# Residual and first product put into PSUM by ScalarE, so that the matmuls add to them

## The chip, the cores and the metric

The kernel runs on one core of a Trainium2 chip. The metric is the device time of one execution in microseconds (us); times are medians of several runs. A traced execution gives the profile: the busy time of TensorE (PE), its weight load (PEld), VectorE (DVE), ScalarE (ACT), GpSimd (POOL), and the DMA queues, of which SyncE (SP) issues nearly all.

## The reference

Two layers over 256 tokens of width 1024. Each layer has a token mixer beside a cross-attention, and then the dense channel mixer with which the change deals:

```python
def layer_norm(x, g, b): ...       # over the last axis
def swiglu(x, w_in, w_out):
    g, u = jnp.split(x @ w_in, 2, axis=-1)
    return (jax.nn.silu(g) * u) @ w_out
for i in range(DEPTH):             # DEPTH = 2
    ...
    x = layer_norm(ALPHA * x + sub, ln_mix_g[i], ln_mix_b[i])
    x = layer_norm(ALPHA * x + swiglu(x, w_ffn_in[i], w_ffn_out[i]), ln_ffn_g[i], ln_ffn_b[i])
```

Everything is float32. w_ffn_in[i] is 1024 x 5632 and w_ffn_out[i] is 2816 x 1024.

## The kernel before

**Tiling.** The 256 tokens are two tiles of 128 (tt = 0, 1). The 2816 hidden columns are eleven chunks of 256. Each float32 operand is split into two parts that TensorE multiplies: the high part is a cast on ScalarE (L240), the low part is the rest, a subtraction on VectorE (L241). Three matmul passes (PASSES) make one product. So each half of a weight unit, 128x1024, costs one cast, one subtraction and its matmuls. Weight units come from memory as 1 MB loads (`raw_...`) through a ring of four; the split halves (`spl_...`) go through a ring of ten.

**Channel mixer.** Class Ffn. PLANS says which chunks are plain ("R", chunk_in) and which pairs of chunks are made with seven products M1 to M7 in Strassen's manner ("S", product). In layer 0 the pairs begin at chunks 2, 4, 6, 8; in layer 1 at 3, 5, 7, 9. A pair needs sums of raw weight blocks: two adds of 128x2048 on VectorE (L195) beside one accumulating load by POOL, and a third add for M4. The names of tiles carry f for layer 0 and g for layer 1.

**A pair, step by step.** M1 is copied by ScalarE from its bank X to SBUF (m1). M5 is copied to m5. When M2 is done in bank Y, VectorE adds it to m1 (L611) and ScalarE applies Silu. M6 is copied to u2, VectorE adds M3 to it (L615) and multiplies it with m1 (L616). M7, again in bank X, is added to m5 by VectorE (L618); after that M4 may overwrite the bank. ScalarE makes sg = Silu(M4) (L621), VectorE multiplies m5 by it (L622). The results m1 and m5 are transposed by TensorE at the next "tp" step (L644), and the transposed tiles tp are split by L240 and L241 into ht (htf, htg), the left operand of the output matmuls (chunk_out, acc_mms) into four accumulator banks fo (fof, fog): two token tiles by two halves of 512 columns.

**LayerNorm.** When a tile's sums are complete, VectorE computes ALPHA*xres + fo into xres (L338), bn_stats of it (L344), the aggregate (L350), adds epsilon (L352); POOL takes the power; two more VectorE operations per piece normalise (L356, L357). In the last tile (last_tile) the sums of the last three chunks go to three extra banks `last`, which VectorE adds to xres (L717), column piece by column piece.

**Order.** TensorE's order is written by hand (manual_schedule; ffn_steps makes it). The orders of the other engines and of SP's queue are set by a scheduler from the whole program, so an edit at one place can move instructions at others.

Of the kernel before, what the change touches and what calls it, by code (L numbers as in the profile page):

```python
# [21 lines left out]
P = 128  # L22
# [8 lines left out]
LAST_PIECES = ((0, 512), (512, 768), (768, 1024))  # L31
PASSES = ((0, 0), (0, 1), (1, 0))
# [195 lines left out]
def build(nc, tc, ins, out):  # L228
    ET = mybir.EngineType
    with (  # L230
# [99 lines left out]
        class LayerNorm:  # L330
            def __init__(self, tt, xres, acc, nm):
                self.tt, self.r, self.acc, self.nm = tt, xres[tt], acc, nm
                self.stats = sm(f"st{nm}{tt}", 18)
                self.n = 0

            def piece(self, i):
                c0, c1 = PIECES[i]
                nc.vector.scalar_tensor_tensor(  # L338
                    self.r[:, c0:c1], self.r[:, c0:c1], ALPHA, self.acc[c0 // 512][:, c0 % 512:c0 % 512 + c1 - c0],
                    ALU.mult, ALU.add)  # L340
                self.sums(c0, c1)

            def sums(self, c0, c1):
# [149 lines left out]
        def acc_mms(acc, lhs, rhs, first, last):  # L493

            for a in range(2):
                for b in range(2 - a):
                    for h in range(2):
                        mm(acc[h], lhs(a), rhs(b, h * 512, h * 512 + 512), first and a == 0 and b == 0, last and a == 1)

        def closing(acc, terms, ln):  # L500

            for p, (c0, c1) in enumerate(PIECES):
                for i, (lhs, rhs) in enumerate(terms):
                    for a in range(2):
                        for b in range(2 - a):
                            mm(acc[c0 // 512][:, c0 % 512:c0 % 512 + c1 - c0], lhs(a), rhs(b, c0, c1),
                               False, i == len(terms) - 1 and a == 1)
                ln.piece(p)
# [24 lines left out]
        class Ffn:  # L533
# [52 lines left out]
            def product(self, c, m):  # L586


                if m == "M1":
                    self.X, self.Y, self.Z = (mm_tile(f"{n}{self.nm}{c}") for n in "XYZ")  # L590
                dst = {"M1": self.X, "M6": self.X, "M7": self.X, "M4": self.X, "M2": self.Y}.get(m, self.Z)
                alone = m in ("M1", "M5", "M2")
# [61 lines left out]
            def run(self, mid=None):  # L654
                for st in ffn_steps(self.l):
# [14 lines left out]
                    elif st[0] == "tp":  # L670
                        if self.pending:
# [10 lines left out]
            def chunk_out(self, c, k, tts):  # L682
                if c == 0 and k == 0:
                    self.alloc()
                for tt in tts:
                    acc_mms(self.acc[tt], *self.term(c, k, tt), c == 0 and k == 0,
                            self.l == 1 and c == NFF - 4 and tt == 1 and k == 1)
# [3 lines left out]
            def end_tile(self, tt, mid=None):  # L691

                for c in range(NFF - 2 if tt == 0 else NFF - 3, NFF - 1):
                    for k in range(2):
                        acc_mms(self.acc[tt], *self.term(c, k, tt), False, False)
# [4 lines left out]
                ln = LayerNorm(tt, self.xres, self.acc[tt], self.nm)  # L700
                closing(self.acc[tt], [self.term(NFF - 1, k, tt) for k in range(2)], ln)
# [4 lines left out]
            def last_tile(self, tt):  # L706

                ln = LayerNorm(tt, self.xres, self.acc[tt], self.nm)
# [313 lines left out]
```

## Time and profile before

| | us |
|---|---|
| median of 3 runs | 566.76 (566.74 to 566.94) |
| the profiled execution, its own time | 567.08 |
| span from its first to its last instruction | 565.4 |
| TensorE busy in it | 554.6 |
| VectorE busy | 499.3 |
| ScalarE busy | 360.6 |

TensorE is busy 98% of the span, at a mean granted clock of 0.995. The share of an engine is a mean over stages; what an edit is worth is read from the stage in which it stands. An instruction's row gives its start and its length; the next instruction of the same engine may start some 0.08 us before the end of the one before it, so a split of 1.22 us takes 1.13 to 1.14 us of the engine's time in a run of splits.

### The profile page before, as it was taken

The page shows a single profiled execution, that of the slowest core. Times are in us where ns is not written, and L with a number is a line of the kernel's source. Part 1 is how long each engine was busy: PE and PEld are TensorE (multiplying, and loading weights), DVE is VectorE, ACT ScalarE, POOL GpSimd, SP SyncE. Part 2 cuts the span into 40 slices and gives each one's busy share as a digit, 9 for nine tenths or more (in the row PEclk, how much of TensorE's full clock was granted, in tenths as well). Part 3 has the DMA queues.
Part 4 walks back from the last instruction along what each step waited for, and adds up shares of the span by engine and source line. Part 5 has one row for each costly group of instructions (what it writes and reads, how often), then busy time and mean ns, then how long its engine had stood idle before and what let it go on. Part 6 is the DMA issues. An engine that isn't in the chain of part 4 may idle for free.

```text
span 565.4 us, 8050 instructions
## 1 busy us (share of the span) xinstructions
PE 554.6 (98%) x3064; PEld 479.4 (85%) x3064; DVE 499.3 (88%) x641; ACT 360.6 (64%) x552; POOL 22.5 (4%) x32
## 2 busy tenths in 40 slices
PE   8999999999999999999999999999999999999994
PEld 8999979888888888888999998788888887888884
DVE  5796989999997999995987887589998997999986
ACT  6765957768664756872475987555676674765820
POOL 2020000000000000000100000000000000000001
PEclk9999999999999999999999999999999999999997
DMA  8995786547866576687476324237367766585602
GB/s 303 410 369 225 248 311 231 204 77 305 214 241 216 139 298 150 228 329 261 152 267 256 144 77 148 85 149 284 90 176 278 206 243 213 137 305 145 222 1 74
DMA packets 21334, 118.88 MB, mean 210 GB/s; under 512 B 2352, under 2 KB 5552, under 8 KB 8880
## 3 DMA queue, kind: packets, MB, share of 16 engines
q1 hardware_dynamic: 19856, 109.72, 52.7%
q0 software_dynamic: 1152, 8.39, 8.2%
q8 instruction: 24, 0.39, 0.3%
q10 hardware_dynamic: 288, 0.26, 0.1%
q14 instruction: 14, 0.11, 0.1%
HBM read 117.31 MB, written 1.05 MB: 209 GB/s over the span
## 4 chain that ended last, share of the span: by engine, by line
PE 85%; DVE 8%; ACT 2%; DMA 2%; issue 2%; SPq 0%; POOLq 0%; ACTq 0%; DVEq 0%
PE fof L264 11%; PE Xf L264 8%; PE fog L264 6%; PE pf L264 6%; PE pg L264 6%; PE Xg L264 5%; PE opc L264 4%; PE opa L264 4%; PE Zf L264 4%; PE qk L264 4%; PE pu L264 3%; PE bv L264 3%; PE pvm L264 3%; PE Zg L264 3%; PE va L264 3%; PE hkm L264 2%
## 5 line engine op out<-in xcount | busy, mean ns | idle before, releaser
L240 ACT CAST spl_s_M<-raw_s 128x1024 fp32r<-128x1024 f32 x112 | 114.8, 1053 | 51.3 <-DVE raw_s L195 37.3
L241 DVE TENSOR_TENSOR spl_s_M<-raw_s,spl_s_M 128x1024 fp32r<-128x1024 f32 x112 | 132.8, 1219 | 5.7 <-ACT spl_s_M L240 5.4
L264 PE MATMUL fof<-spl_w,htf 128*128 128x512 f32 x264 | 63.8, 392 | 0.0
L264 PEld LDWEIGHTS fof<-spl_w,htf 128*128 128x128 f32 x264 | 49.0, 188 | 10.0
L264 PE MATMUL fog<-spl_w,htg 128*128 128x512 f32 x228 | 55.3, 392 | 0.0
L195 DVE TENSOR_TENSOR raw_s<-raw_s,raw_s 128x2048 f32<-128x2048 f32 x24 | 54.9, 2286 | 0.2
L241 DVE TENSOR_TENSOR spl_w<-raw_w,spl_w 128x1024 fp32r<-128x1024 f32 x44 | 53.0, 1218 | 1.5 <-ACT spl_w L240 1.5
L240 ACT CAST spl_w<-raw_w 128x1024 fp32r<-128x1024 f32 x44 | 45.5, 1052 | 6.6 <-PE fog L264 1.9
L264 PEld LDWEIGHTS fog<-spl_w,htg 128*128 128x128 f32 x228 | 42.4, 188 | 8.6
L264 PE MATMUL qk<-x2T,spl_qk 128*128 128x256 f32 x288 | 36.7, 285 | 0.0
L264 PEld LDWEIGHTS qk<-x2T,spl_qk 128*128 128x128 f32 x288 | 35.2, 192 | 0.0
L264 PE MATMUL opc<-spl_o,mix 128*128 128x512 f32 x96 | 23.5, 397 | 0.0
L264 PE MATMUL Xf<-spl_s_M,SfM 128*128 128x512 f32 x96 | 23.1, 389 | 0.0
L264 PE MATMUL Xg<-spl_s_M,x3T 128*128 128x512 f32 x96 | 22.8, 391 | 0.3 <-DVE m5g L618 0.3
L264 PE MATMUL Zg<-spl_s_M,SgM 128*128 128x512 f32 x96 | 23.1, 389 | 0.0
L264 PE MATMUL Xg<-spl_s_M,SgM 128*128 128x512 f32 x96 | 23.1, 389 | 0.0
L264 PE MATMUL Zf<-spl_s_M,SfM 128*128 128x512 f32 x96 | 23.1, 389 | 0.0
L264 PE MATMUL Xf<-spl_s_M,x1T 128*128 128x512 f32 x96 | 22.6, 389 | 0.0
L264 PE MATMUL opa<-spl_o,mix 128*128 128x512 f32 x96 | 22.5, 392 | 0.0
L264 PEld LDWEIGHTS Xg<-spl_s_M,x3T 128*128 128x128 f32 x96 | 17.9, 188 | 4.5 <-DVE m5g L618 0.8
L264 PEld LDWEIGHTS Xf<-spl_s_M,SfM 128*128 128x128 f32 x96 | 18.0, 188 | 3.8
L264 PEld LDWEIGHTS Xg<-spl_s_M,SgM 128*128 128x128 f32 x96 | 18.0, 188 | 3.7
(240 smaller groups left out, 1101.9 us busy)
## 6 DMA issues: line engine op xcount, KB each, us to landing
raw_s<-in_w SPq DMA_DIRECT2D x32, 1024.0 KB, 4.8
raw_w<-in_w SPq DMA_DIRECT2D x22, 1024.0 KB, 5.6
raw_o<-in_w SPq DMA_DIRECT2D x8, 1024.0 KB, 6.7
raw_s<-in_w POOLq DMA_DIRECT2D x8, 1024.0 KB, 8.2
raw_r_A<-in_w SPq DMA_DIRECT2D x6, 1024.0 KB, 4.8
raw_r_B<-in_w SPq DMA_DIRECT2D x6, 1024.0 KB, 4.8
raw_qk<-in_w SPq DMA_DIRECT2D x6, 1024.0 KB, 5.6
raw_u<-in_w SPq DMA_DIRECT2D x3, 1024.0 KB, 8.6
```

The costliest lines, as they stand in the source:

```text
L195: self.nc.vector.tensor_add(self.raw[parts[0]], self.raw[parts[0]], self.raw[parts[1]])
L240: nc.scalar.copy(hi, src)
L241: nc.vector.tensor_sub(lo, src, hi.bitcast(F32))
L264: nc.tensor.matmul(o, lhsT, rhs, start=start, stop=stop, skip_group_check=on)
```

## The change

Three edits. First, at the first "tp" step of a channel mixer, ScalarE writes ALPHA*xres into the four accumulator banks (eight operations of 128x512 in all); every output matmul then adds to what lies there, and LayerNorm reads its sums from the banks, not from xres. The six additions of L338 that served the channel mixers, and five more of last_tile (L710, L717), are gone; last_tile adds into the banks themselves, pieces in another order. Second, ScalarE copies M1 into the bank of M2, the matmuls of M2 add to it, and Silu reads the bank: the eight adds of L611 are gone. In the new code the tile that M1, M6, M7 and M4 write is named Y, and M2's X. Third, transposes are written as plain matmul instructions with flags, four in a group; their number stays.

```diff
+            def src(self, c0, c1):
+                return self.part(c0, c1) if self.seeded else self.r[:, c0:c1]
...
             def sums(self, c0, c1):
-                nc.vector.bn_stats(self.stats[:, 6 * self.n:6 * self.n + 6], self.r[:, c0:c1])
+                nc.vector.bn_stats(self.stats[:, 6 * self.n:6 * self.n + 6], self.src(c0, c1))
...
-                    nc.vector.scalar_tensor_tensor(r[:, sl], r[:, sl], mv[:, 0:1], gb[:, 0, sl], ALU.subtract, ALU.mult)
+                    nc.vector.scalar_tensor_tensor(r[:, sl], self.src(c0, c1), mv[:, 0:1], gb[:, 0, sl], ALU.subtract, ALU.mult)
...
-            def alloc(self):
+            def seed(self):
                 self.acc = [[acc_tile(f"fo{self.nm}{tt}{h}") for h in range(2)] for tt in range(2)]
+                for tt in range(2):
+                    for h in range(2):
+                        nc.scalar.mul(self.acc[tt][h], self.xres[tt][:, h * 512:(h + 1) * 512], ALPHA)
...
-                alone = m in ("M1", "M5", "M2")
+                alone = m in ("M1", "M5")
...
                 if m == "M1":
-                    self.m1 = kept("m1", self.X)
+                    nc.scalar.copy(self.Y, self.X)
...
                 elif m == "M2":
-                    nc.vector.tensor_add(self.m1, self.m1, self.Y)
-                    nc.scalar.activation(self.m1, self.m1, AF.Silu)
+                    self.m1 = work_tile(f"m1{self.nm}{c}")
+                    nc.scalar.activation(self.m1, self.Y, AF.Silu)
...
-                            nc.tensor.transpose(tp[:, k, tt * P:(tt + 1) * P], hs[tt][:, k * P:(k + 1) * P], ident)
+                            nc.tensor.matmul(tp[:, k, tt * P:(tt + 1) * P], hs[tt][:, k * P:(k + 1) * P], ident,
+                                             start=k + tt == 0, stop=k + tt == 2, is_transpose=True, skip_group_check=True)
...
             def last_tile(self, tt):
-                ln = LayerNorm(tt, self.xres, self.acc[tt], self.nm)
-                for h, (c0, c1) in enumerate(PIECES):
-                    nc.vector.scalar_tensor_tensor(ln.r[:, c0:c1], ln.r[:, c0:c1], ALPHA, self.acc[tt][h], ALU.mult, ALU.add)
+                ln = LayerNorm(tt, self.xres, self.acc[tt], self.nm, True)
                 terms = [self.term(c, k, tt) for c in range(NFF - 3, NFF) for k in range(2)]
-                for c0, c1 in LAST_PIECES:
-                    t = mm_tile(f"last{c0}")[:, :c1 - c0]
+                for c0, c1 in LAST_ORDER:
                     for i, (lhs, rhs) in enumerate(terms):
                         for n, (a, b) in enumerate(PASSES):
-                            mm(t, lhs(a), rhs(b, c0, c1), i == 0 and n == 0, i == len(terms) - 1 and n == 2)
-                    nc.vector.tensor_add(ln.r[:, c0:c1], ln.r[:, c0:c1], t)
+                            mm(ln.part(c0, c1), lhs(a), rhs(b, c0, c1), False, i == len(terms) - 1 and n == 2, True)
                     ln.sums(c0, c1)
```

LAST_ORDER is (512, 768), (0, 512), (768, 1024).

The scheduler's orders change with it. First place: VectorE at the end of layer 0's pair 8 and the start of plain chunk 10. Before, from the add into u2 to the last product of m5 (L622):

```order
L615 TENSOR_TENSOR u2f8_2227<-u2f8_2227,Zf8_2081 128x512
L241 TENSOR_TENSOR spl_w0_7_0_2271<-raw_w0_7_2119,spl_w0_7_0_2271 128x1024
L616 SCALAR_TENSOR_TENSOR m1f8_2100<-m1f8_2100,u2f8_2227 128x512
L241 TENSOR_TENSOR spl_s0_8_M4_0_2287<-raw_s0_8_21_2064,spl_s0_8_M4_0_2287 128x1024
L241 TENSOR_TENSOR spl_s0_8_M4_1_2296<-raw_s0_8_21_2064,spl_s0_8_M4_1_2296 128x1024
L618 TENSOR_TENSOR m5f8_2153<-m5f8_2153,Xf8_2079 128x512
L241 TENSOR_TENSOR spl_r0_10_A_0_2310<-raw_r0_10_A_2258,spl_r0_10_A_0_2310 128x1024
L241 TENSOR_TENSOR spl_w0_7_1_2344<-raw_w0_7_2119,spl_w0_7_1_2344 128x1024
L241 TENSOR_TENSOR spl_r0_10_A_1_2361<-raw_r0_10_A_2258,spl_r0_10_A_1_2361 128x1024
L241 TENSOR_TENSOR spl_r0_10_B_0_2378<-raw_r0_10_B_2260,spl_r0_10_B_0_2378 128x1024
L622 SCALAR_TENSOR_TENSOR m5f8_2153<-m5f8_2153,sgf8_2305 128x512
```

Now:

```order
L629 TENSOR_TENSOR u2f8_2227<-u2f8_2227,Zf8_2082 128x512
L242 TENSOR_TENSOR spl_r0_10_A_0_2310<-raw_r0_10_A_2258,spl_r0_10_A_0_2310 128x1024
L630 SCALAR_TENSOR_TENSOR m1f8_2188<-m1f8_2188,u2f8_2227 128x512
L242 TENSOR_TENSOR spl_w0_7_1_2344<-raw_w0_7_2119,spl_w0_7_1_2344 128x1024
L242 TENSOR_TENSOR spl_r0_10_A_1_2361<-raw_r0_10_A_2258,spl_r0_10_A_1_2361 128x1024
L632 TENSOR_TENSOR m5f8_2153<-m5f8_2153,Yf8_2081 128x512
L242 TENSOR_TENSOR spl_r0_10_B_0_2378<-raw_r0_10_B_2260,spl_r0_10_B_0_2378 128x1024
L242 TENSOR_TENSOR spl_r0_10_B_1_2393<-raw_r0_10_B_2260,spl_r0_10_B_1_2393 128x1024
L242 TENSOR_TENSOR spl_w0_8_0_2416<-raw_w0_8_2262,spl_w0_8_0_2416 128x1024
L242 TENSOR_TENSOR spl_w0_8_1_2425<-raw_w0_8_2262,spl_w0_8_1_2425 128x1024
L242 TENSOR_TENSOR spl_w0_9_0_2444<-raw_w0_9_2347,spl_w0_9_0_2444 128x1024
L636 SCALAR_TENSOR_TENSOR m5f8_2153<-m5f8_2153,sgf8_2305 128x512
```

The add of M7 into m5 (L618, now L632) stood ahead of the four splits for chunk 10 and w0_7; it now stands behind three of them. The last product of m5 (now L636) stood behind one further split, and now stands behind five, the last of which is of w0_9.

Second place: VectorE at the start of layer 1's pair 9, where m5g7 is finished and htg7, htg8 are the transposed results of pair 7. Before:

```order
L618 TENSOR_TENSOR m5g7_4616<-m5g7_4616,Xg7_4542 128x512
L241 TENSOR_TENSOR spl_w1_7_0_4831<-raw_w1_7_4758,spl_w1_7_0_4831 128x1024
L195 TENSOR_TENSOR raw_s1_9_11_4756<-raw_s1_9_11_4756,raw_s1_9_12_4760 128x2048
L241 TENSOR_TENSOR spl_s1_9_M5_0_4848<-raw_s1_9_11_4756,spl_s1_9_M5_0_4848 128x1024
L622 SCALAR_TENSOR_TENSOR m5g7_4616<-m5g7_4616,sgg7_4772 128x512
L241 TENSOR_TENSOR spl_s1_9_M5_1_4857<-raw_s1_9_11_4756,spl_s1_9_M5_1_4857 128x1024
L241 TENSOR_TENSOR spl_s1_9_M2_0_4868<-raw_s1_9_21_4762,spl_s1_9_M2_0_4868 128x1024
L241 TENSOR_TENSOR htg7_4804<-tpg7_4775,htg7_4804 128x512
L241 TENSOR_TENSOR htg8_4811<-tpg8_4776,htg8_4811 128x512
L241 TENSOR_TENSOR spl_s1_9_M2_1_4877<-raw_s1_9_21_4762,spl_s1_9_M2_1_4877 128x1024
```

Now:

```order
L632 TENSOR_TENSOR m5g7_4613<-m5g7_4613,Yg7_4541 128x512
L242 TENSOR_TENSOR spl_w1_7_0_4827<-raw_w1_7_4755,spl_w1_7_0_4827 128x1024
L196 TENSOR_TENSOR raw_s1_9_11_4753<-raw_s1_9_11_4753,raw_s1_9_12_4757 128x2048
L242 TENSOR_TENSOR spl_s1_9_M5_0_4844<-raw_s1_9_11_4753,spl_s1_9_M5_0_4844 128x1024
L636 SCALAR_TENSOR_TENSOR m5g7_4613<-m5g7_4613,sgg7_4769 128x512
L242 TENSOR_TENSOR spl_s1_9_M5_1_4853<-raw_s1_9_11_4753,spl_s1_9_M5_1_4853 128x1024
L242 TENSOR_TENSOR spl_s1_9_M2_0_4864<-raw_s1_9_21_4759,spl_s1_9_M2_0_4864 128x1024
L242 TENSOR_TENSOR spl_s1_9_M2_1_4873<-raw_s1_9_21_4759,spl_s1_9_M2_1_4873 128x1024
L242 TENSOR_TENSOR spl_s1_9_M3_0_4884<-raw_s1_9_22_4761,spl_s1_9_M3_0_4884 128x1024
L242 TENSOR_TENSOR htg7_4800<-tpg7_4772,htg7_4800 128x512
L242 TENSOR_TENSOR htg8_4807<-tpg8_4773,htg8_4807 128x512
L242 TENSOR_TENSOR spl_s1_9_M3_1_4893<-raw_s1_9_22_4761,spl_s1_9_M3_1_4893 128x1024
```

The splits of htg7 and htg8 stood behind the first split of M2; they now stand behind the second split of M2 and the first of M3 as well.

Third place: SP's queue of loads before layer 1's pair 7. Before:

```order
L181 DMA raw_w1_5_4525<-in_w 128x2048
L181 DMA raw_s1_7_22_4529<-in_w 128x2048
L181 DMA raw_s1_7_11_4521<-in_w 128x2048
L181 DMA raw_s1_7_21_4527<-in_w 128x2048
L181 DMA raw_w1_6_4582<-in_w 128x2048
```

Now:

```order
L182 DMA raw_w1_5_4523<-in_w 128x2048
L182 DMA raw_s1_7_11_4519<-in_w 128x2048
L182 DMA raw_s1_7_22_4527<-in_w 128x2048
L182 DMA raw_s1_7_21_4525<-in_w 128x2048
L182 DMA raw_w1_6_4579<-in_w 128x2048
```

The load of block 11 now goes ahead of that of block 22. Before pair 9 of the same layer it is the other way: block 11 was issued first and now goes behind blocks 12 and 22.

## Rows read from the trace of the kernel before

**Rows 1.** The page, first part: busy time, share and count by engine.
```profile
PE 554.6 (98%) x3064; PEld 479.4 (85%) x3064; DVE 499.3 (88%) x641; ACT 360.6 (64%) x552; POOL 22.5 (4%) x32
```

**Rows 2.** Windows: stretch, its length, busy us of PE, PEld, DVE, ACT, POOL, clock, DMA.
```profile
400.00:500.00 100.00, 99.67 (x453) 82.24 (x452) 93.78 (x84) 65.22 (x77) 2.59 (x3) 1.00 0.64 203
500.00:540.00 40.00, 40.00 (x184) 33.16 (x184) 38.77 (x39) 26.80 (x33) 0.88 (x1) 1.00 0.63 204
540.00:565.40 25.40, 17.43 (x96) 14.97 (x94) 18.47 (x34) 1.25 (x3) 1.86 (x2) 0.89 0.12 42
```

**Rows 3.** TensorE's waits: line, whom it waited for, us in total, times, longest.
```profile
PE Xg L264 <- DVE m5g L618: 0.3, 1, 0.3
```

**Rows 4.** The chain that ended last, from 555 us: start, length, what.
```profile
557.44 0.02 issue
557.46 0.43 DVE xres L717
...
557.92 0.44 DVE stg L344
```

**Rows 5.** VectorE's groups by line and shape: busy us, mean ns of one.
```profile
L241 DVE TENSOR_TENSOR spl_s_M<-raw_s,spl_s_M 128x1024 fp32r<-128x1024 f32 x112 | 132.8, 1219 | 5.7 <-ACT spl_s_M L240 5.4
L195 DVE TENSOR_TENSOR raw_s<-raw_s,raw_s 128x2048 f32<-128x2048 f32 x24 | 54.9, 2286 | 0.2
...
L356 DVE SCALAR_TENSOR_TENSOR xres<-xres,mvf,gb0ffn 128x512 f32<-128x512 f32 x4 | 2.8, 744 | 0.0
...
L611 DVE TENSOR_TENSOR m1f<-m1f,Yf 128x512 f32<-128x512 f32 x4 | 2.7, 684 | 0.3 <-PE Yf L264 0.3
...
L338 DVE SCALAR_TENSOR_TENSOR xres<-xres,fof 128x512 f32<-128x512 f32 x4 | 2.7, 680 | 2.8 <-PE fof L264 2.8
```

**Rows 6.** VectorE's timeline, layer 0, end of pair 8: start, us, line.
```profile
239.94 0.68 DVE L618 TENSOR_TENSOR m5f<-m5f,Xf 128x512 f32<-128x512 f32 x1
...
241.67 1.22 DVE L241 TENSOR_TENSOR spl_w<-raw_w,spl_w 128x1024 fp32r<-128x1024 f32 x1
...
245.51 0.69 DVE L622 SCALAR_TENSOR_TENSOR m5f<-m5f,sgf 128x512 f32<-128x512 f32 x1 [0.36 <-ACT sgf L621]
```

**Rows 7.** TensorE's timeline there: M4 of pair 8, and the first transpose of m5.
```profile
241.74 2.88 PE L264 MATMUL Xf<-spl_s_M,x1T 128*128 128x512 f32 x12
...
247.29 0.27 PE L644 MATMUL tpf<-ident,m5f 128*128 128x128 f32 x1
```

**Rows 8.** SP's timeline there: the loads of w0_9 and w0_10 are issued.
```profile
242.91 1.46 SPq L181 DMA_DIRECT2D raw_w<-in_w  x2
```

**Rows 9.** ScalarE's timeline there: the casts of w0_9.
```profile
248.78 2.01 ACT L240 CAST spl_w<-raw_w 128x1024 fp32r<-128x1024 f32 x2
```

**Rows 10.** The page's sixth part: KB of a load, median us to landing.
```profile
raw_w<-in_w SPq DMA_DIRECT2D x22, 1024.0 KB, 5.6
```

**Rows 11.** VectorE's timeline, layer 1, start of pair 9.
```profile
507.13 0.68 DVE L618 TENSOR_TENSOR m5g<-m5g,Xg 128x512 f32<-128x512 f32 x1
...
512.35 1.23 DVE L241 TENSOR_TENSOR spl_s_M<-raw_s,spl_s_M 128x1024 fp32r<-128x1024 f32 x1 [1.20 <-ACT spl_s_M L240]
513.49 0.68 DVE L622 SCALAR_TENSOR_TENSOR m5g<-m5g,sgg 128x512 f32<-128x512 f32 x1
514.09 2.35 DVE L241 TENSOR_TENSOR spl_s_M<-raw_s,spl_s_M 128x1024 fp32r<-128x1024 f32 x2
516.36 1.28 DVE L241 TENSOR_TENSOR htg<-tpg,htg 128x512 fp32r<-128x512 f32 x2
```

**Rows 12.** TensorE's timeline there: M7's end, M4 and M1, first transpose of m5, outputs.
```profile
503.69 2.65 PE L264 MATMUL Xg<-spl_s_M,SgM 128*128 128x512 f32 x11
...
508.90 5.61 PE L264 MATMUL Xg<-spl_s_M,x3T 128*128 128x512 f32 x24
...
514.46 0.27 PE L644 MATMUL tpg<-ident,m5g 128*128 128x128 f32 x1
...
515.14 5.73 PE L264 MATMUL fog<-spl_w,htg 128*128 128x512 f32 x24
```

More of the change, by code (lines that the diff above doesn't have):

```diff
@@ L31 @@
 LAST_PIECES = ((0, 512), (512, 768), (768, 1024))
+LAST_ORDER = ((512, 768), (0, 512), (768, 1024))
 PASSES = ((0, 0), (0, 1), (1, 0))
@@ L330, in build, with __init__ @@
         class LayerNorm:
-            def __init__(self, tt, xres, acc, nm):
-                self.tt, self.r, self.acc, self.nm = tt, xres[tt], acc, nm
+            def __init__(self, tt, xres, acc, nm, seeded=False):
+                self.tt, self.r, self.acc, self.nm, self.seeded = tt, xres[tt], acc, nm, seeded
                 self.stats = sm(f"st{nm}{tt}", 18)
@@ L337, in piece, with part @@
                 c0, c1 = PIECES[i]
-                nc.vector.scalar_tensor_tensor(
-                    self.r[:, c0:c1], self.r[:, c0:c1], ALPHA, self.acc[c0 // 512][:, c0 % 512:c0 % 512 + c1 - c0],
-                    ALU.mult, ALU.add)
+                if not self.seeded:
+                    nc.vector.scalar_tensor_tensor(
+                        self.r[:, c0:c1], self.r[:, c0:c1], ALPHA, self.part(c0, c1), ALU.mult, ALU.add)
                 self.sums(c0, c1)
+            def part(self, c0, c1):
+                return self.acc[c0 // 512][:, c0 % 512:c0 % 512 + c1 - c0]
+            def src(self, c0, c1):
+                return self.part(c0, c1) if self.seeded else self.r[:, c0:c1]
             def sums(self, c0, c1):
-                nc.vector.bn_stats(self.stats[:, 6 * self.n:6 * self.n + 6], self.r[:, c0:c1])
+                nc.vector.bn_stats(self.stats[:, 6 * self.n:6 * self.n + 6], self.src(c0, c1))
                 self.n += 1
@@ L491, in mem_k, with acc_mms @@
             return ka, klm
-        def acc_mms(acc, lhs, rhs, first, last):
+        def acc_mms(acc, lhs, rhs, first, last, on=False):
             for a in range(2):
@@ L497, in acc_mms, with closing @@
                     for h in range(2):
-                        mm(acc[h], lhs(a), rhs(b, h * 512, h * 512 + 512), first and a == 0 and b == 0, last and a == 1)
-        def closing(acc, terms, ln):
+                        mm(acc[h], lhs(a), rhs(b, h * 512, h * 512 + 512), first and a == 0 and b == 0, last and a == 1, on)
+        def closing(acc, terms, ln, on=False):
             for p, (c0, c1) in enumerate(PIECES):
@@ L506, in closing @@
                             mm(acc[c0 // 512][:, c0 % 512:c0 % 512 + c1 - c0], lhs(a), rhs(b, c0, c1),
-                               False, i == len(terms) - 1 and a == 1)
+                               False, i == len(terms) - 1 and a == 1, on)
                 ln.piece(p)
@@ L589, in product @@
                 if m == "M1":
-                    self.X, self.Y, self.Z = (mm_tile(f"{n}{self.nm}{c}") for n in "XYZ")
+                    self.Y, self.X, self.Z = (mm_tile(f"{n}{self.nm}{c}") for n in "XYZ")
                 dst = {"M1": self.X, "M6": self.X, "M7": self.X, "M4": self.X, "M2": self.Y}.get(m, self.Z)
-                alone = m in ("M1", "M5", "M2")
+                alone = m in ("M1", "M5")
                 for x in range(2):
@@ L670, in run @@
                     elif st[0] == "tp":
+                        if not self.acc:
+                            self.seed()
                         if self.pending:
@@ L682, in chunk_out @@
             def chunk_out(self, c, k, tts):
-                if c == 0 and k == 0:
-                    self.alloc()
                 for tt in tts:
-                    acc_mms(self.acc[tt], *self.term(c, k, tt), c == 0 and k == 0,
-                            self.l == 1 and c == NFF - 4 and tt == 1 and k == 1)
+                    acc_mms(self.acc[tt], *self.term(c, k, tt), False, False, True)
                 if 1 in tts:
@@ L694, in end_tile @@
                     for k in range(2):
-                        acc_mms(self.acc[tt], *self.term(c, k, tt), False, False)
+                        acc_mms(self.acc[tt], *self.term(c, k, tt), False, False, True)
                     if tt == 1:
@@ L699, in end_tile @@
                     mid()
-                ln = LayerNorm(tt, self.xres, self.acc[tt], self.nm)
-                closing(self.acc[tt], [self.term(NFF - 1, k, tt) for k in range(2)], ln)
+                ln = LayerNorm(tt, self.xres, self.acc[tt], self.nm, True)
+                closing(self.acc[tt], [self.term(NFF - 1, k, tt) for k in range(2)], ln, True)
                 if tt == 1:
```

2 lines of the change are left out of this document (1 added, 1 removed).

## The prediction, written before the result was known

> **What bounds the kernel now.** I read the busy times first: TensorE works 554.6 us of the span of 565.4 [rows 1]. Then the windows, where the idle time lies: 0.33 us between 400 and 500 us, none between 500 and 540, and 7.97 us after 540, in the tail behind the last matmul [rows 2]. So TensorE bounds the body. VectorE is next, 93.78 us of 100 and 38.77 of 40 in the pair chunks [rows 2]; the body works only because VectorE hands over each operand just in time. The list of TensorE's waits has one that belongs to the edited code: 0.3 us on the add of M7 into m5 in layer 1 [rows 3]. Last, the chain that ended last shows what the tail is made of: behind the last matmul an add (L717), bn_stats (L344), and what follows them [rows 4].
>
> This says what the change can give. Time comes from the tail, and from that one wait; VectorE's saved work is worth something only where TensorE waits for VectorE. And it says what can be lost: any operand that a new order of VectorE brings later than TensorE wants it.
>
> **The tail.** The last piece's add goes: 0.43 us and its issue gap of 0.02, so 0.45 [rows 4]. In its place bn_stats reads a PSUM bank and one piece of L356 on the path does too. No row shows bn_stats from PSUM. From below, nothing is lost: the add L338, which reads a bank, takes 680 ns, and L356 of the same shape, all in SBUF, 744 [rows 5], so reading a bank isn't visibly dearer. From above, I allow that difference of 64 ns the other way, on both instructions: 0.13 us. The nearer row is L338, the same kind of instruction with a bank as operand, so I take 0.44, bounds 0.32 to 0.45. The Trainium skill (Perfetto Trace Analysis, section Optimizing Scalar/DVE Operations) gives VectorE an access overhead of about 60 ns on SBUF and about 125 ns on PSUM; by it, as an estimate, the tail would give 0.32 and the sum below would be 0.12 us higher. The trace doesn't bear that out: its instruction with a bank operand is the shorter one.
>
> **Removed from VectorE in the body.** Eight adds of 0.68 us (L611), some 0.6 us of VectorE's time in each pair, and six additions L338 of 0.68 [rows 5]. This moves no end by itself, since TensorE waits for nothing there; it lets VectorE run ahead. Added on ScalarE are eight seeds, at most 0.7 us each by the nearest 128x512 rows [rows 5]; ScalarE is idle a third of the time [rows 1]. M1's copy now has a reader on TensorE, M2. What covers it is the output matmuls and M5 that stand between: M1 ends at 514.51 in the pair that we look at, and 5.7 us of outputs alone follow before M5 [rows 12]. I put both at nothing; if the copy were later than its cover, M2 would wait for the difference. The transposes keep count and shape: nothing.
>
> **The new order of VectorE.** Here lie the costs. Every split stands for 1.13 to 1.14 us of VectorE's time, an operation of 128x512 for 0.6, a raw add for 2.2 to 2.3 [rows 5, 11].
>
> *Layer 0, end of pair 8.* Before, the add of M7 into m5 ended at 240.62 and M4, which overwrites the bank, began at 241.74 [rows 6, 7]: 1.1 us to spare. Now three splits more stand ahead of it, 3.4 us. From that goes 0.6 for the pair's own add L611, and what VectorE has gained in the three pairs before, between nothing and 3 x 0.6 = 1.8 us. So the add ends between 243.4 and 241.6; I take two thirds of the gain, 242.2. M4 then waits 0.5 us (0 to 1.7). After the add come five splits and the product of m5: 5 x 1.13 + 0.69 = 6.3 us, so m5 is ready at 248.5. The first transpose of m5, which stood at 247.29 [rows 7], stands at 247.8 after the first wait: another 0.8 us. Before, the product ended at 246.20 [rows 6]. The last of the five splits also needs its load: w0_9 was issued at 242.91, right behind the split of w0_7 that frees its buffer (it ended at 242.89) [rows 6, 8]. In the new order that split ends two units of work (one split and the add, 1.7 us) ahead of the end of the add, so at 240.5; 5.6 us later the load has landed [rows 10], then the cast, 1.05 [rows 9], the split and the product: 248.9 at the latest, no different answer. Together 1.3 us, with bounds of 0.6 (all gain, so 247.9 against 247.29) and 2.4 (no gain).
>
> *Layer 1, start of pair 9.* The second dozen of the 24 output matmuls that begin at 515.14 needs htg7; it starts at 518.0 [rows 12]. Before, htg7 was done at 517.04: two splits stood between the product of m5 (513.49) and it [rows 11]. Now two more stand there: 514.09 + 4 x 1.135 + 0.68 = 519.3, if the add of M7 starts at 507.13 as before. That add can't start before M7 ends, 506.34 [rows 12], 0.8 us earlier; from there on to htg7 VectorE's own work is a closed row (w1_7's split, the raw add, the cast that it waits for, the splits). So htg7 comes between 518.5 and 519.3, and TensorE waits 0.5 to 1.3 us. If the load of block 11, now last of three in SP's queue, comes late, 0.2 us more; I take 1.1. This is the firmest of the costs: running ahead can't help, since M7 itself holds the row back.
>
> *Elsewhere.* In the other pairs, too, a split or a raw add has moved ahead of a product of m5 or stands later. From below nothing, from above one split, 1.2 us [rows 5]; most of it lies in slack of the same size that VectorE's saved 0.6 us enlarges, so I take 0.3.
>
> *Layer 1, pair 7.* Block 11 is now loaded ahead of block 22, so the raw add behind which the add of M7 stood isn't late, and the wait of 0.3 us [rows 3] goes: 0.3 (0 to 0.33).
>
> **Sum.** +1.3 +1.1 +0.3 -0.3 -0.44 = +1.96 us, bounds +0.3 and +4.6. The profiled execution took 567.08 us, so 569.0. It stood 0.32 above the median of the runs, 566.76; the forecast for the median is 568.7, slower by 0.35%. The bounds give 567.1 to 571.4.
>
> **Rivals.**
> *The waits don't come (no change).* VectorE runs farther ahead than I grant: the end of pair 8 costs nothing, and htg7 is in time. For it speaks that VectorE loses 0.6 us of work in each pair. Against it, that the row from M7's end to htg7 holds no slack that could be given up. It decides at 518.0 in layer 1: if htg7 is ready by then, only the gains are left, 566.76 - 0.44 - 0.3 = 566.0. With one of the two waits of about 1.2 us, 567.2. All from 565.7 to 567.8 is no change.
>
> *Loads become the wait (slower still).* Block 11 of pair 9 is issued behind two others, and its landing sets M1's split; blocks of pair 8 likewise. A 1 MB load takes 5.6 us in the median [rows 10]; if it comes one such load later than now, the splits ahead of M1 and M5 slip by more than their lead, and 1.5 us or so more are lost: 570.2.
>
> *Faster.* That the seeded banks and freed VectorE give more than 0.2%, 1.13 us. All that TensorE waits in the body and the tail's add come to 0.33 + 0.45 = 0.78 us, so there must be a gain that I don't see, such as a shorter way from bn_stats to the store. Then 565.4.
>
> **Chances and range.** Slower by two waits as summed, 0.45; slower still through loads, 0.10; no change, 0.40; faster, 0.05. A difference under 0.2% can't be told from none in this kernel. Slower by over 0.2% means above 567.9: 0.55. The likeliest case alone has 567.9 to 570.0. With the case of no change the range is 566.0 to 570.1, since both of them hold most of the chance.
>
> **What would show it.** In the profile after, L611, the L338 of the channel mixers and L717 are gone, and the tail from the last matmul to the last instruction is shorter by 0.3 to 0.45 us. TensorE's list of waits has new entries: transposes and M4's matmuls at the first plain chunk after pair 8, on VectorE's m5; and output matmuls in layer 1's pair 9 on htg. The wait in pair 7 is gone. If TensorE's idle time between 200 and 540 us is not larger than before, the prediction is wrong, and VectorE's lead is what I undervalued.

## The result, and the profile after

The changed kernel takes 571.22 us (median of 6 runs, 569.29 to 572.61) against 566.82 (566.59 to 567.33) for the kernel before: ratio 1.0068, 95% interval 1.0055 to 1.0081. A ratio here is estimated over all the runs and need not be the quotient of the two medians, which is 1.0078. The changed kernel is slower, by about twice what was forecast (4.4 us between the medians, 3.9 by the ratio, 1.9 forecast). Its median lies above the range of the prediction, though inside the bounds of its sum (567.1 to 571.4). Its runs also lie wider apart, 3.3 us instead of 0.7. The profiled execution took 571.14 us, its span 569.4 us, 4.0 more than before.

The page's first part, as [rows 1]:

```profile
PE 555.9 (98%) x3064; PEld 479.0 (84%) x3064; DVE 488.9 (86%) x622; ACT 365.5 (64%) x560; POOL 20.3 (4%) x32
```

The arithmetic came out as written: VectorE has 10.4 us less to do, ScalarE 4.9 more, TensorE the same number of matmuls. The time went into waits. The windows, as [rows 2] (stretch, length, busy us of PE, PEld, DVE, ACT, POOL, clock, DMA):

```profile
400.00:500.00 100.00, 99.23 (x450) 81.42 (x449) 94.75 (x87) 66.44 (x79) 2.59 (x3) 1.00 0.62 202
500.00:540.00 40.00, 40.00 (x182) 33.16 (x182) 36.14 (x32) 26.81 (x32) 0.88 (x1) 1.00 0.64 204
```

In layer 1's pairs TensorE is idle 0.77 us of 100 where it was 0.33, and in pair 9 it is still never idle: the clock is 1.00 in both, so it isn't the clock. Where it waits, the list of TensorE's waits says (line, whom it waited for, us in total, times, longest), beside [rows 3]:

```profile
PE tpf L659 <- DVE m5f L636: 1.8, 1, 1.8
...
PE Zg L265 <- DVE htg L242: 0.8, 2, 0.5
PE Zf L265 <- DVE htf L242: 0.6, 2, 0.3
...
PE pf L265 <- ACT Aa L379: 0.3, 1, 0.3
```

The entry of [rows 3] is gone, and three kinds of wait are new. The first, the transposes' wait for m5 at chunk 10, was forecast. The other two were not: **M5 (Z) waits for VectorE's split of ht**, four times; and layer 0's **first gated products (pf) wait for a copy on ScalarE** that has nothing to do with the change's formulas.

What each costs is read from the distance between two instructions of TensorE, before and after, since the list counts only the part of a gap that a semaphore explains. M5 in pair 4 of layer 0: TensorE's timeline of the kernel before (start, us, line; outputs, then M5),

```profile
155.46 2.98 PE L264 MATMUL fof<-spl_w,htf 128*128 128x512 f32 x12
158.28 2.88 PE L264 MATMUL Zf<-spl_s_M,SfM 128*128 128x512 f32 x12
```

and of the changed one:

```profile
156.21 2.98 PE L265 MATMUL fof<-spl_w,htf 128*128 128x512 f32 x12
159.47 3.02 PE L265 MATMUL Zf<-spl_s_M,SfM 128*128 128x512 f32 x12 [0.28 <-DVE htf L242]
```

2.82 us became 3.26: 0.44 lost. The same distance gives 0.50 in pair 6 (2.84, 3.34), 0.41 in pair 5 of layer 1 (2.85, 3.26) and 0.67 in pair 7 (2.82, 3.49). VectorE's timeline of the changed kernel at pair 4 shows what M5 waits for:

```profile
154.72 0.69 DVE L636 SCALAR_TENSOR_TENSOR m5f<-m5f,sgf 128x512 f32<-128x512 f32 x1
155.32 3.49 DVE L242 TENSOR_TENSOR spl_s_M<-raw_s,spl_s_M 128x1024 fp32r<-128x1024 f32 x3
158.73 1.28 DVE L242 TENSOR_TENSOR htf<-tpf,htf 128x512 fp32r<-128x512 f32 x2
```

The first of the two ht splits ends about 159.4, and M5 starts at 159.47. M5 does not read ht. It is written into the bank whose transposes that split reads: in the compiled program, from which the bank numbers below are taken, four banks serve X, Y, Z and tp in turn, and a tile gets its bank at its first write. Before, pair 4 had M1 in bank 6, the two tp in 7 and 4, M5 in 5, and M2, written last, took the bank 7 of tp2 (the transposes of chunk 2). Now M1's copy writes M2's bank (6) before M5 starts; M1's is 4, the tp lie in 7 and 5, and the only bank left for M5 is tp2's, which VectorE must have read first.

Chunk 10 in layer 0. VectorE's timeline, as [rows 6]:

```profile
242.85 0.68 DVE L632 TENSOR_TENSOR m5f<-m5f,Yf 128x512 f32<-128x512 f32 x1
...
245.72 2.35 DVE L242 TENSOR_TENSOR spl_w<-raw_w,spl_w 128x1024 fp32r<-128x1024 f32 x2
249.48 1.23 DVE L242 TENSOR_TENSOR spl_w<-raw_w,spl_w 128x1024 fp32r<-128x1024 f32 x1 [1.40 <-ACT spl_w L241]
250.62 0.69 DVE L636 SCALAR_TENSOR_TENSOR m5f<-m5f,sgf 128x512 f32<-128x512 f32 x1
```

ScalarE's, as [rows 9], and SP's, as [rows 8]:

```profile
248.40 1.05 ACT L241 CAST spl_w<-raw_w 128x1024 fp32r<-128x1024 f32 x1 [3.87 <-DMA raw_w<-in_w]
249.35 0.59 ACT L635 ACTIVATE sgf<-Yf 128x512 f32<-128x512 f32 x1
```

```profile
241.87 1.42 SPq L182 DMA_DIRECT2D raw_w<-in_w  x2
```

TensorE's, as [rows 7]:

```profile
243.80 2.90 PE L265 MATMUL Yf<-spl_s_M,x1T 128*128 128x512 f32 x12
...
249.26 0.27 PE L659 MATMUL tpf<-ident,m1f 128*128 128x128 f32 x1
251.36 0.33 PE L659 MATMUL tpf<-ident,m5f 128*128 128x128 f32 x1 [1.82 <-DVE m5f L636]
```

The load of w0_9 was issued at 241.87 and its cast began at 248.40, 6.5 us later; ScalarE sat idle for it 3.87 us, with Silu(M4) queued behind the cast, and VectorE 1.40, with the product of m5 queued behind the split. The transposes of m1 and m5, 0.11 us apart where nothing is missing (as the experiment on this load shows them), are 2.10 apart: 1.99 lost. [rows 7] has the second of them before the change. The add of M7 ended at 243.53, in time for M4 at 243.80.

The tail in the chain that ended last (start, length, what), as [rows 4]:

```profile
555.00 6.99 PE fog L265 x42
561.99 0.02 issue
562.01 0.45 DVE stg L352
```

From the last matmul to the end it is 569.4 - 561.99 = 7.41 us, and was 565.4 - 557.44 = 7.96: 0.55 won. The bn_stats takes 0.45 from a bank, 0.44 before from SBUF.

So far that makes M5's waits 0.44 + 0.50 + 0.41 + 0.67 = +2.02; chunk 10 +1.99; pf +0.49 (shown with its experiments); pair 7's old wait -0.49; tail -0.55: 3.46 of the 4.0 us. The rest is found by going on to the next group of matmuls. The first matmul after such a wait takes 0.50 us instead of 0.39, so that M5's twelve take 3.02 us instead of 2.88 (the rows above), and from the outputs ahead of M5 to those behind it (in pair 4 from 155.46 to 161.00 before, from 156.21 to 162.32 now) the four places lose 0.57, 0.64, 0.58 and 0.82, 2.61 in all. By the same measure pair 7's old wait was 0.62, and M5 of pair 8, which isn't in the list, loses 0.15. The start of the kernel, where the first products wait for their loads, gives 0.22. And there is a gain that the lists do not show, at layer 0's last LayerNorm, where TensorE transposes its result. Before and after:

```profile
284.09 1.29 PE L365 MATMUL ptb<-ident,xres 128*128 128x128 f32 x8
```

```profile
288.08 1.03 PE L373 MATMUL ptb<-ident,xres 128*128 128x128 f32 x8
```

Before, VectorE's last scaling (L357) ended at 284.60, when these transposes had begun; now it ends 1.4 us ahead of them. From the products in front of them to those behind it is 8.43 us before, 8.10 now, 8.09 with the first edit alone and 8.42 with the second alone, so the gain of 0.33 is the first edit's. With these the sum is 2.61 + 1.99 + 0.49 + 0.15 + 0.22 - 0.62 - 0.33 - 0.55 = 3.96.

### The profile page after: what moved, and what is told of

It is laid out like the page before. It is cut to its first block, busy times and chain, and to the rows that moved or that the text cites. A ratio compares the mean times of both kernels' runs of the same rounds, so it can differ in the third digit from the quotient of the medians.

```text
span 569.4 us, 8073 instructions
## 1 busy us (share of the span) xinstructions
PE 555.9 (98%) x3064; PEld 479.0 (84%) x3064; DVE 488.9 (86%) x622; ACT 365.5 (64%) x560; POOL 20.3 (4%) x32
## 4 chain that ended last, share of the span: by engine, by line
PE 70%; DVE 16%; ACT 4%; issue 4%; DMA 4%; SPq 0%; ACTq 0%; DVEq 0%
PE fog L265 7%; PE fof L265 6%; PE pg L265 6%; DVE spl_s_M L242 6%; PE pf L265 5%; PE opc L265 4%; PE opa L265 4%; PE Yg L265 4%; PE qk L265 4%; DVE raw_s L196 3%; PE pu L265 3%; PE Zg L265 3%; PE bv L265 3%; PE Yf L265 3%; PE Zf L265 3%
## 5 line engine op out<-in xcount | busy, mean ns | idle before, releaser
L265 PE MATMUL fog<-spl_w,htg 128*128 128x512 f32 (+1 forms) x282 | 63.7, 378 | 0.0
L265 PEld LDWEIGHTS fog<-spl_w,htg 128*128 128x128 f32 x282 | 50.2, 188 | 9.4
L265 PE MATMUL Yf<-spl_s_M,SfM 128*128 128x512 f32 x96 | 23.1, 389 | 0.0
L265 PE MATMUL Yg<-spl_s_M,SgM 128*128 128x512 f32 x96 | 23.1, 389 | 0.0
L265 PE MATMUL Yg<-spl_s_M,x3T 128*128 128x512 f32 x96 | 22.6, 389 | 0.0
L265 PE MATMUL Yf<-spl_s_M,x1T 128*128 128x512 f32 x96 | 22.6, 389 | 0.0
L265 PEld LDWEIGHTS Zg<-spl_s_M,SgM 128*128 128x128 f32 x96 | 17.9, 188 | 5.3 <-DVE htg L242 1.6
L265 PEld LDWEIGHTS Zf<-spl_s_M,SfM 128*128 128x128 f32 x96 | 17.8, 188 | 5.3 <-DVE htf L242 1.7
L265 PEld LDWEIGHTS Yg<-spl_s_M,x3T 128*128 128x128 f32 x96 | 18.0, 188 | 3.8
```

What stands on the lines that cost most here:

```text
L265: nc.tensor.matmul(o, lhsT, rhs, start=start, stop=stop, skip_group_check=on)
```

## The experiments

All run beside the kernel before; its median was 566.90 (19 runs) beside the first four, 566.86 (30) beside the next four and 567.04 (23) beside the last two. "Ratio" is to those runs, with the 95% interval.

**Each edit alone.** First the seeds and LayerNorm from the banks, with M1 and M2 as before (the transposes stay in the new form):

```diff
-                    self.Y, self.X, self.Z = (mm_tile(f"{n}{self.nm}{c}") for n in "XYZ")
+                    self.X, self.Y, self.Z = (mm_tile(f"{n}{self.nm}{c}") for n in "XYZ")
-                    nc.scalar.copy(self.Y, self.X)
+                    self.m1 = kept("m1", self.X)
...
+                    nc.vector.tensor_add(self.m1, self.m1, self.Y)
```

> Edit 1 alone: seeds by ScalarE, LayerNorm reads the banks, last_tile adds into them; M1 goes to SBUF as before and VectorE adds M2 to it. The orders of VectorE, ScalarE and SP in the pairs are those of before. Theory A (the loss is made of waits that the M1 edit's order and banks bring): the first chunk of layer 0 starts 0.5 us later behind the seeds, the tail is 0.5 us shorter, so 566.8 us, no change within 0.2%. Rival B (matmuls that add to seeded banks are slower, since TensorE's busy time rose by 1.3 us with the change): 568 us or more, and the output matmuls' mean above 392 ns.

Measured: 566.43 us (566.15 to 566.94, 12 runs), ratio 0.9992 (0.9984 to 1.0001). Then M1's copy into M2's bank alone, with the accumulators and LayerNorm as before:

```diff
-                for tt in range(2):
-                    for h in range(2):
-                        nc.scalar.mul(self.acc[tt][h], self.xres[tt][:, h * 512:(h + 1) * 512], ALPHA)
...
-                ln = LayerNorm(tt, self.xres, self.acc[tt], self.nm, True)
+                ln = LayerNorm(tt, self.xres, self.acc[tt], self.nm)
```

> Edit 2 alone: M1 is copied into M2's bank, transposes in groups; accumulators and LayerNorm as before. The orders in the pairs are those of the changed kernel. Theory A: all the large waits are here: 2.0 us at the first transposes of chunk 10 in layer 0, 2.5 us at M5 of four pairs, less 0.6 us in pair 7 of layer 1; 570.5 to 571.5 us. Rival B: 567 to 569 us, since the seeds are what costs.

Measured: 571.57 us (569.49 to 572.92, 6 runs), ratio 1.0074 (1.0055 to 1.0093). The whole loss, and the scatter, belong to the edit on M1 and M2; its trace has the waits of m5 (1.7) and of Z (2.2 in all), and not that of pf. Both kernels have the transposes in the new form, and the first loses nothing, so the third edit costs nothing that shows. The orders within the pairs are those of before in the first and those of the changed kernel in the second.

**The load in the chain at chunk 10.** The changed kernel, with the cast and the split of w0_9's first half issued behind Silu(M4) and the product of m5; on ScalarE and VectorE nothing else moves.

```diff
-        self.split(hl[:, 0, :n], hl[:, 1, :n], raw)
+        if key in self.behind:
+            si, vi = self.behind[key]
+            with self.tc.issue_after(si), self.tc.issue_after(vi):
+                self.split(hl[:, 0, :n], hl[:, 1, :n], raw)
...
+                    if (self.l, c) == (0, 8):
+                        stream.behind["w0_9", 0] = si.ins, vi.ins
```

> The changed kernel with one cast and one split moved: those of w0_9_0 are issued behind Silu(M4) and the last product of m5 in layer 0's pair 8; all other orders are the same. Theory A (the load of w0_9 stands in the chain to m5): m5 is ready at about 248.8 us on the trace's clock against transposes at 249.4, the wait of 1.8 us goes, about 569.2 us, and the runs scatter less than the 3.3 us of the changed kernel, since that wait takes its length from a load. Rival B (VectorE has no lead, the wait moves to the next handover): less than 0.7 us is gained.

Measured: 568.80 us (568.50 to 569.45, 8 runs), ratio 1.0031 (1.0020 to 1.0041): 2.4 us less than the changed kernel by the medians, against 2.0 forecast, and the runs lie within 0.95 us. VectorE's timeline there:

```profile
247.87 0.69 DVE L642 SCALAR_TENSOR_TENSOR m5f<-m5f,sgf 128x512 f32<-128x512 f32 x1
250.01 3.70 DVE L247 TENSOR_TENSOR spl_w<-raw_w,spl_w 128x1024 fp32r<-128x1024 f32 x3 [1.46 <-ACT spl_w L246]
```

and TensorE's:

```profile
249.14 0.27 PE L667 MATMUL tpf<-ident,m1f 128*128 128x128 f32 x1
249.25 0.27 PE L667 MATMUL tpf<-ident,m5f 128*128 128x128 f32 x1
```

VectorE still waits 1.46 us for the load, but now m5 is done at 248.56, before its transpose wants it at 249.25, and TensorE doesn't wait. Moving one split behind its neighbour, and its cast likewise, takes more than half of the loss.

**M5's bank, a first attempt.** The changed kernel with its three tiles named in another order, so that M5's comes first.

```diff
-                    self.Y, self.X, self.Z = (mm_tile(f"{n}{self.nm}{c}") for n in "XYZ")
+                    self.Z, self.X, self.Y = (mm_tile(f"{n}{self.nm}{c}") for n in "ZXY")
```

> The changed kernel with the three banks of a pair taken in the order Z, X, Y instead of Y, X, Z; the orders of VectorE, ScalarE, SP and POOL are the same to the instruction. Theory A (M5 waits because its bank Z is the one that the first transposed tile of the pair before held, until VectorE has split it): Z now gets a bank that Silu(M4) frees, the waits of M5 in pairs 4 and 6 of layer 0 and 5 and 7 of layer 1 go, 2.5 us in all, about 568.8 us. Rival B (M2's bank now is the one that waits, and M1's copy into it with it): the time stays at 570.5 to 572 us, with waits at M2.

Measured: 573.16 us (569.49 to 574.49, 6 runs), ratio 1.0102 (1.0077 to 1.0127). It did not do what it was for: a bank is given at the first write, not where the tile is named, so banks and orders came out as in the changed kernel, and M5's waits are there (Z 1.0 + 0.6 in the list). It is the changed kernel a second time, and beside these runs the load experiment is 4.4 us less, not 2.4. Its profiled run was its fastest, 569.49, and in that one the load had landed within 4.9 us (issued at 241.53, cast at 246.41) and m5 cost 0.3 us in the list, not 1.8. That fits the scatter; why its median lies 1.9 us above that of the same orders was not settled.

**M5's bank by a later first write.** The kernel of the load experiment, and M1's copy issued behind m5's copy in the five pairs that have the wait or are near it. M5 now gets its bank first, and M2 takes tp's, as before the change.

```diff
+                late = c in (4, 5, 6, 7, 8)
...
-                    nc.scalar.copy(self.Y, self.X)
+                    if not late:
+                        nc.scalar.copy(self.Y, self.X)
...
+                    mi = nc.scalar.copy(self.m5, self.Z)
+                    if late:
+                        with tc.issue_after(mi.ins):
+                            nc.scalar.copy(self.Y, self.X)
```

> Base: the changed kernel with the load of w0_9 taken out of the chain (568.80). Added: in pairs 4, 6 and 8 of layer 0 and 5 and 7 of layer 1, M1's copy into M2's accumulator is issued behind m5's copy, so that M2's bank is taken after M5's. Theory (a bank is held from its first write, so the early copy pushed M5 into the bank whose transposes VectorE has still to split): TensorE's waits of M5 for htf and htg (2.4 us in the changed kernel's trace) go, and the median falls to about 566.3 to 566.9. Rival 1 (M5 is late because VectorE's queue is in a new order, whatever the bank): 568.5 to 569. Rival 2 (M2 now waits for the late copy, some 0.6 us a pair in five pairs): 569 to 572, with a wait of TensorE on Y for ScalarE.

Measured: 566.34 us (565.58 to 567.40, 11 runs), ratio 0.9980 (0.9967 to 0.9993): 2.46 less than without it. No wait of Z, and none of M2 for the copy. But the edit also changed VectorE's order, with ht's split one place earlier in those pairs, so by itself it doesn't tell the bank from the order. The next two do.

**The order alone, the bank alone.** First the old banks with the early split: in pairs 6 and 8 of layer 0 and 7 of layer 1 the addition and the first split for M6 go behind ht's split; in pairs 4 and 5 ht's split stays behind three others.

```diff
+            with self.first(key, ("s0_6", "s0_8", "s1_7")):
+                self.nc.vector.tensor_add(self.raw[parts[0]], self.raw[parts[0]], self.raw[parts[1]])
...
+            with self.first(key, ("s0_4", "s0_6", "s0_8", "s1_5", "s1_7")):
+                self.nc.vector.tensor_sub(hl[:, 1, :n], raw, hl[:, 0, :n].bitcast(F32))
```

> Base: the changed kernel with the load of w0_9 taken out of the chain (568.80), M1's copy early, so that M5 keeps the bank of the transposes. Added: in pairs 6 and 8 of layer 0 and 7 of layer 1 VectorE splits the two ht tiles ahead of the addition for M6 instead of behind it (in pairs 4 and 5 the order cannot be brought about, there the split stays third). Theory (the wait needs both, the shared bank and the late split): M5's waits of pairs 6 and 7 (0.49 and 0.81 us) go, those of pairs 4 and 5 (0.44 and 0.40) stay: 567.3 to 567.8. Rival 1 (the shared bank alone makes M5 late): 568.5 to 569. Rival 2 (M6 is late in place of ht, for its addition now comes behind): a wait of TensorE on M6's split, 568 or more.

Measured: 567.21 us (566.62 to 569.30, 12 runs), ratio 1.0011 (1.0000 to 1.0021), 0.1 under what the theory gave. The list of TensorE's waits in its trace:

```profile
PE Yg L280 <- ACT u2g L631: 0.7, 1, 0.7
...
PE Zg L280 <- DVE htg L256: 0.3, 1, 0.3
PE Zf L280 <- DVE htf L256: 0.3, 1, 0.3
```

One wait of Z is left in each layer, in pairs 4 and 5, and those of 6 and 7 are gone with the same banks. (M7 waited once for the copy of u2, which moved too; that is the price of this order, and the trace is of the slowest of its runs.) Then the late copy with the late split: ahead of the transposes the program asks for M6's first half, and in pairs 4, 6, 5 and 7 VectorE has ht's split in the place that it has in the changed kernel.

```diff
+                key = (f"s{self.l}_{self.pending[0][0][0] + 2}", "M6", 0)
+                if key[0] in ("s0_4", "s0_6", "s0_8", "s1_5", "s1_7"):
+                    stream.get(*key)
                 for (c, hs), tp in zip(self.pending.pop(0), self.turn.pop(0)):
```

> Base: e6_both (566.34), M1's copy late, so that M5's bank is not that of the transposes. Added: VectorE splits the ht tiles of pairs 4 and 6 of layer 0 and 5 and 7 of layer 1 behind the first split or the addition for M6, as the changed kernel does. Theory (the wait needs both): no wait of M5 although ht is split late, 566.2 to 566.8. Rival (the late split alone makes M5 or the outputs late): 568 or more, with M5's waits of about 0.4 to 0.8 us as before.

Measured: 566.34 us (565.79 to 567.67, 11 runs), ratio 0.9990 (0.9981 to 0.9999). VectorE's timeline at pairs 4 and 6, and TensorE's:

```profile
158.05 1.28 DVE L247 TENSOR_TENSOR htf<-tpf,htf 128x512 fp32r<-128x512 f32 x2
...
189.09 1.28 DVE L247 TENSOR_TENSOR htf<-tpf,htf 128x512 fp32r<-128x512 f32 x2
```

```profile
158.35 1.98 PE L271 MATMUL Zf<-spl_s_M,SfM 128*128 128x512 f32 x8
...
189.20 1.07 PE L271 MATMUL Zf<-spl_s_M,SfM 128*128 128x512 f32 x4
```

A single split of ht takes 0.68 us, so M5 starts 0.4 us before the first one has ended in pair 4, and 0.6 before in pair 6. With another bank it doesn't care. So the wait needs both, the shared bank and the late split, and either remedy takes it away. (Both edits also moved two loads and a few operations of ScalarE; the lists of waits show nothing of it but M7's wait and 0.2 us at a transpose, both in the first.)

**The seeds.** The kernel of the late copy, and layer 0's four seeds issued behind the last copy of the attention's transposed output on ScalarE:

```diff
-                        nc.scalar.mul(self.acc[tt][h], self.xres[tt][:, h * 512:(h + 1) * 512], ALPHA)
+                        with (tc.issue_after(stream.kept) if self.l == 0 else nullcontext()):
+                            nc.scalar.mul(self.acc[tt][h], self.xres[tt][:, h * 512:(h + 1) * 512], ALPHA)
```

> e6_both, and the four seeds of layer 0 issued behind the last copy of the attention's transposed output on ScalarE. Theory (the seeds hold up that copy, and the copy the bank of the first gated products, 0.49 us): 0.4 to 0.5 below e6_both, that is 565.8 to 566.4, which is the kernel before or up to 1 us better. Rival (the bank is late for another reason, the seeds are hidden): the same as e6_both within 0.15, with the wait of pf for ScalarE still 0.3 or more.

Measured: 565.41 us (565.10 to 567.29, 11 runs), ratio 0.9975 (0.9963 to 0.9988), 0.93 below the same without it and under the 565.8 to 566.4 expected. The same edit on the first edit alone:

> The kernel before with the first edit alone (seeded output accumulators, LayerNorm from PSUM; 566.43), and the four seeds of layer 0 issued behind the last copy of the attention's transposed output on ScalarE. Theory (the seeds cost 0.49 us in front of layer 0's first gated products): 565.9 to 566.1, which is under the kernel before by 0.1 to 0.2 per cent. Rival: 566.3 to 566.6, with the wait of pf for ScalarE as it was.

Measured: 565.79 us (565.33 to 566.54, 11 runs), ratio 0.9979 (0.9969 to 0.9989), 0.64 below, and 0.1 under the expected. The mechanism, in ScalarE's and TensorE's timelines. Before:

```profile
101.24 1.08 ACT L371 COPY Aa<-pta 128x512 f32<-128x512 f32 x2
```

```profile
101.88 2.33 PE L264 MATMUL pf<-spl_r_A,x1T 128*128 128x512 f32 x9
```

After the change:

```profile
97.45 0.59 ACT L552 ACTIVATE fof<-xres 128x512 f32<-128x512 f32 x1
...
98.71 0.59 ACT L552 ACTIVATE fof<-xres 128x512 f32<-128x512 f32 x1
...
101.96 1.08 ACT L379 COPY Aa<-pta 128x512 f32<-128x512 f32 x2
```

```profile
102.60 1.67 PE L265 MATMUL pf<-spl_r_A,x1T 128*128 128x512 f32 x6 [0.34 <-ACT Aa L379]
```

The first of the two copies ends some 0.6 us after their start and frees the bank for pf: in the kernel before that is just when TensorE comes to it. Two seeds of 0.59 us were put ahead of it, beside 0.5 us of idle time there; the copy came 0.72 later and pf 0.72, of which 0.22 is that execution's later start. With the seeds behind the copies the entry of pf is gone from the list of waits in both kernels. Both gained somewhat more than 0.49; their ranges overlap with those of the kernels without it, so the excess isn't shown to be real. Both beat the kernel before, and which of them is the better is not told apart.

**Why pair 9 cost nothing.** The kernel of the load experiment, where the first half of chunk 7's outputs in layer 1 takes the low part of htg7 first:

```diff
-                    acc_mms(self.acc[tt], *self.term(c, k, tt), False, False, True)
+                    acc_mms(self.acc[tt], *self.term(c, k, tt), False, False, True,
+                            (1, 0) if (self.l, c, k) == (1, 7, 0) else (0, 1))
```

> Base: the changed kernel with the load of w0_9 taken out of the chain (568.80). Added: the outputs of chunk 7 of layer 1, first half of its rows, take the low part of htg7 first instead of last. Theory (the predicted 1.1 us did not come because the first four of the six products of each tile use the high part, which ScalarE's cast gives 1.4 us before VectorE's split ends): TensorE waits 0.7 to 0.9 us there for VectorE, and the median rises to 569.4 to 569.8. Rival (VectorE's split ends in time anyway): no such wait, 568.6 to 569.0.

Measured: 569.51 us (569.19 to 569.75, 8 runs), ratio 1.0040 (1.0028 to 1.0052): 0.71 more. The changed kernel's VectorE at this place, beside [rows 11], its ScalarE, and its TensorE, beside [rows 12]:

```profile
517.92 4.63 DVE L242 TENSOR_TENSOR spl_s_M<-raw_s,spl_s_M 128x1024 fp32r<-128x1024 f32 x4
522.47 1.28 DVE L242 TENSOR_TENSOR htg<-tpg,htg 128x512 fp32r<-128x512 f32 x2
```

```profile
521.14 1.07 ACT L241 CAST htg<-tpg 128x512 fp32r<-128x512 f32 x2
```

```profile
519.67 5.73 PE L265 MATMUL fog<-spl_w,htg 128*128 128x512 f32 x24
```

and TensorE's outputs in this experiment:

```profile
517.15 3.01 PE L271 MATMUL fog<-spl_w,htg 128*128 128x512 f32 x12
520.69 3.02 PE L271 MATMUL fog<-spl_w,htg 128*128 128x512 f32 x12 [0.53 <-DVE htg L247]
```

In the changed kernel the outputs began at 519.67, so the second dozen came up at about 522.4, and VectorE's split of htg7 ended at 523.15. Yet nothing waited, the 24 took 5.73 us as before: of the six matmuls of a tile the first four use the high part, which ScalarE's cast had given by 521.7; the low part is wanted four matmuls later, 0.9 us, at 523.3. Taken first, it costs what the trace shows here, 3.54 us from dozen to dozen instead of 2.8.

## Why the prediction was wrong, point by point

**The sign was right, the size half.** +1.96 us were summed, 4.06 came in the profiled executions.

**"I put both at nothing", and 0.3 for all that lies "Elsewhere": this is the step that failed.** For M1's copy the prediction asked only who reads it (M2, well covered: true, M2 never waited in the changed kernel). It did not ask what the copy writes. It takes M2's bank before M5 starts, so M5 gets a bank that VectorE still reads, 2.02 us in four pairs up to M5's start and 2.61 up to the outputs behind it. The late splits that make it bite were seen, as "a raw add has moved ahead", and were set against slack that the bank had taken away. The seeds, too, were covered only by ScalarE's mean idle time; at their place the slack of ScalarE's copy was nil, 0.49 us. In the same paragraph, VectorE's removed work "moves no end by itself": at layer 0's last LayerNorm it did, by 0.33 us the other way.

**Layer 0, end of pair 8: right mechanism, 1.3 forecast, 1.99 measured.** M4 did not wait (0.5 forecast): the add ended 0.27 us before it. The product's wait was larger (0.8 forecast): not the five splits decided but w0_9's load. The prediction had the load as the later end, 248.9, and called it no different answer; with it the place would have come to 1.6. It took 6.5 us instead of the 5.6 of [rows 10], and ScalarE's Silu stood behind its cast as well.

**Layer 1, pair 9: "the firmest of the costs", 1.1 forecast, nothing measured.** VectorE's row came as described: four splits stand between m5's product and htg7, which came 0.75 us after the second dozen began (0.5 to 1.3 forecast). The step that failed is that the second dozen "needs htg7; it starts at 518.0": that is when the first use of htg7 begins, which is of the high part. The low part is needed 0.9 us later, and the reversed order brings the wait back.

**Pair 7, -0.3 forecast, -0.49 measured: the number came, not by the reason given.** The prediction had a raw add that was late for its load. In the kernel before, the raw add waits for nothing: it stands in a row that is late because VectorE waited 2.49 us for ScalarE's copy of u2. VectorE's timeline before:

```profile
470.12 0.69 DVE L615 TENSOR_TENSOR u2g<-u2g,Zg 128x512 f32<-128x512 f32 x1 [2.49 <-ACT u2g L603]
...
475.02 2.29 DVE L195 TENSOR_TENSOR raw_s<-raw_s,raw_s 128x2048 f32<-128x2048 f32 x1
477.22 0.68 DVE L618 TENSOR_TENSOR m5g<-m5g,Xg 128x512 f32<-128x512 f32 x1
```

and after:

```profile
479.37 0.68 DVE L632 TENSOR_TENSOR m5g<-m5g,Yg 128x512 f32<-128x512 f32 x1
```

The add of M7 ended at 477.90 and M4 began at 477.95; now it ends at 480.05 and M4 begins at 481.79. In the new order three splits stand ahead of the add into u2 instead of behind it, and fill the time in which the copy is awaited. That the right number came was luck. No run changes the order of the loads alone.

**Tail, -0.44 forecast, -0.55 measured.** This was right. bn_stats from a bank costs 0.01 us more in its row, so the lower bound (0.32) was too cautious. The Trainium skill (Perfetto Trace Analysis, section Optimizing Scalar/DVE Operations), by whose overhead for PSUM the tail would, as an estimate, have given 0.32, is not borne out by these rows. The 0.1 more in the tail stands between the small add and the last scaling (from the end of L352 to L357 it was 1.10 us in the chain, and the same two, now L360 and L365, are 0.97 apart); its cause was not tried.

**The rivals.** "The waits don't come" fell; the load did become a wait, as the second rival said, though at chunk 10, not in pair 9. The third, that the banks give a gain, is true of the first edit once its seeds stand elsewhere: 0.9979. Of the "gain that I don't see" that it spoke of, 0.33 us lies at the LayerNorm, which the list of waits did not show.

## What to carry to other kernels

When an operation is put into a PSUM tile earlier than the first matmul, ask which bank it takes and from whom: with four banks for X, Y, Z and two transposes, one write moved ahead can make the next product wait for whoever still reads the bank that is left. Before an operand's lateness is priced, find the matmul that reads that very part: of a split operand the low part is wanted later than the high one. And where a scheduler puts a split of a freshly loaded weight ahead of a link of the chain between engines, the load's landing is in the chain; moving the split and its cast one place took 2.4 us and most of the scatter.

## What was not expected of the hardware

A 1 MB load of the same weight, w0_9, at the same place took between 4.9 us or less and 7.2 us to the start of its cast (issued at 241.53, 241.87 and 241.75 us, cast at 246.41, 248.40 and 248.93 in the traces of three kernels). With this load in the chain a kernel's runs differed by 3.3 us, without it by 0.95.

The start of the kernel varies in the same way. In the trace of the late copy (567.40 us, the slowest of its runs) the list of waits has

```profile
PE va L271 <- ACT spl_v L246: 1.9, 2, 1.4
```

for the first products, which wait for casts of the first loads, and in that of the bank experiment (566.26 us) 0.2. That one stretch is as large as all that is at stake in the better versions, so they are told apart by medians of eleven runs, not by one trace.
